# A two-layer diffusion backbone on one core: where the conditioning columns are summed

## The chip, the cores and the metric

One core of a Trainium2 chip (trn2) runs the whole program in one launch. The metric is the device time of one execution in microseconds, as the median of several runs. Less is better. Differences under 0.2% count as no change.

## What is computed

Two layers over 256 context tokens and 256 latent tokens of width 1024. Each layer normalises the tokens, shifts and scales them by conditioning columns, mixes them (attention, a gated delta network, a recurrent unit), merges the three branches, normalises and shifts again, and ends with a product-key expert layer. The conditioning columns are a matrix times two vectors, one for the latent and one for the context tokens:

```python
def adaln(cond, w, b):
    m = (jax.nn.silu(cond) @ w + b)[:, None, :]
    return jnp.split(m, N_MOD, axis=-1)

def modulate(h, shift, scale):
    return h * (1.0 + scale) + shift
...
for l in range(DEPTH):
    ml = adaln(c, w_ada[l], b_ada[l])
    mc = adaln(c_ctx[None, :], w_ada[l], b_ada[l])
    hl = modulate(rmsnorm(xl, norm1_g[l]), ml[0], ml[1])
    hc = modulate(rmsnorm(xc, norm1_g[l]), mc[0], mc[1])
    yc, yl = token_mixer(hc, hl, rope, l, need_ctx, w_in[l], ...)
    xl = xl + ml[2] * yl
```

`w_ada` is 1024 by 6144 for each layer. All of it is fp32. In the delta network each head pair needs the inverses of unit triangular matrices, and these are computed in the mixers too.

## The kernel before

**Layout.** Channels lie on the 128 partitions, tokens on the free axis. A product with a weight matrix goes by weight tiles of 128x1024 (`tblock`): a DMA brings the tile (`wraw`, three buffers), ScalarE rounds it to `wh`, VectorE forms the rest `wl` (line 97), and TensorE does 24 matmuls, three for each of eight chunks (lines 101 to 103).

**Conditioning.** One call of `ada` is called a block here. It makes 512 of the 6144 outputs of a layer for both vectors. It loads four tiles of 128x1024 fp32 (512 KB each) into `wraw`, does eight TensorE matmuls in which 32 columns of the padded vectors are the stationary side and 512 weight columns the moving side (line 185, spread over four groups of output partitions), copies the 128x512 result from PSUM with ScalarE (line 187), folds and turns it into columns with four small matmuls (line 190), and adds the bias (line 192). There are 24 blocks. Ten of them stand outside the mixers: four ahead of the first mixer, two ahead of the second, two behind each merge. Fourteen stand in the mixers, ten in layer 0 and four in layer 1.

**The mixers.** `mixer` weaves three streams of units: `g`, the delta network in four groups of two heads; `x`, the recurrent and the attention heads; and `f`, merge gates and conditioning blocks taken in turn. The table `RATE` says how many units of `x` and `f` follow each unit of `g`. The units are recorded in that order, and a scheduler then fixes the order of each engine's instructions. At run time every engine goes through its list in order, and so does the queue of DMAs issued from SyncE (SP).

**An inversion.** Each group of the delta network has one (`unit_inverse`). It writes diagonal 32x32 pieces of `W` to DRAM and reads them back in another layout (lines 677 and 681). Then come 60 small VectorE instructions, each of which needs the one before (lines 688 and 690). The result goes through DRAM again (lines 693 and 696) into `X`. Only then can `gdn_levels` start, whose first TensorE instructions are transposes of `X` (line 715). There are eight inversions, four in each layer. In what follows an inversion's chain is the stretch from its first to its last of the 60 instructions. The whole inversion is the stretch from the last product with `W` ahead of it (lines 594 and 595) to the first transpose of line 715.

Of the kernel before, what the change touches and what calls it, by code (L numbers as in the profile page):

```python
# [13 lines left out]
F32 = mybir.dt.float32  # L14
# [5 lines left out]
ALU = mybir.AluOpType  # L20
# [3 lines left out]
P = 128  # L24
# [15 lines left out]
class Net:  # L40
# [45 lines left out]
    th, nacc, nmm, l = None, 0, 0, 0  # L86
# [88 lines left out]
    def ada(self, l, b):  # L175
# [15 lines left out]
        m = slice(4 * b, 4 * b + 4)  # L191
        self.V.tensor_tensor(self.mods[:, l, m], pt, self.bada[:, l, m].unsqueeze(2).to_broadcast([P, 4, 2]), ALU.add)


    def norm_sums(self, pool, x, t0, ks):

        self.r = lambda shape=None, dt=F32: self.t(pool, shape or [P, NTOK], dt, "hr", 8)
        if ks[0] == 0:
            self.nss = self.acc()
        for k in ks:  # L200
            self.ssq(x[:, k, t0:], self.nss[:8, :NTOK - t0], self.selR[:, 7:15], k == 0, k == 7)
# [24 lines left out]
    def mixer(self, l, need):  # L226
        nc, V, S, T, I = self.nc, self.V, self.S, self.T, self.I
        self.l, self.need = l, need
        self.T0 = 0 if need else NC
        self.mgd = self.tc.dram_tile([P, 24, NTOK], F32, name=self.nm("mg"))  # L230
        self.ysd = [self.tc.dram_tile([P, 8, NTOK], F32, name=self.nm(f"ys{k}")) for k in range(3)]
        with ExitStack() as es:
            pool = lambda name: es.enter_context(self.tc.tile_pool(name=self.nm(name), bufs=1, reuse_waits="tile"))
            mp, ring = pool("mx"), pool("ring")
            self.r = lambda shape=None, dt=F32: self.t(ring, shape or [P, NTOK], dt, "t" + self.th, self.RING[self.th])
            self.rg = lambda: self.t(ring, [P, 4, P], F32, "rg", 4)
            self.th = "g"
            self.gdn_gates(mp, l)
            gp = pool("gdn")
            aes = ExitStack()  # L240
            ap = self.wextra = aes.enter_context(self.tc.tile_pool(name=self.nm("att"), bufs=1, reuse_waits="tile"))
            self.gated = set()
            gs = [lambda j=j: self.merge_gate(ring, l, j) for j in (*range(16, 24), *range(16))]
            ad = [lambda a=a: self.ada(*a) for a in ([(0, b) for b in range(4, 10)] + [(1, b) for b in range(4)] if l == 0 else [(1, b) for b in range(6, 10)])]
            g = self.gdn(gp, l)
            x = self.chain(*(u for h in range(8) for u in (self.lru_chunk(l, h), self.att_head(ap, l, h))),
                           self.merge_early(aes, pool, ring, l))
            f = self.chain(*(self.calls(us[i:i + 1]) for i in range(24) for us in (gs, ad)))
            self.weave(g, x, f)
            self.th = self.wextra = None  # L250

# [1180 lines left out]
```

## Time and profile before

| | |
|---|---|
| median of 3 runs | 4547.12 us (4546.77 to 4556.1) |
| the profiled execution | 4536.66 us |
| its span, first to last instruction | 4535.0 us |
| TensorE matmul busy | 4283.0 us, 94% |
| VectorE busy | 3214.4 us, 71% |
| ScalarE busy | 2348.0 us, 52% |
| first mixer, last instruction of its fourth inversion | 943.5 us |
| second mixer, its four inversions | 2737.5 to 3429.5 us |

The views used below are the page itself, the groups of instructions by line, windows (busy time of each engine in a stretch, its number of instructions, and the granted clock of TensorE as a share of full speed, where 1.00 is 2.4 GHz and 0.50 is 1.2 GHz), and the timeline. PE is TensorE's matmuls, PEld its weight loads, DVE VectorE, ACT ScalarE, POOL GpSimd.

### The profile page before, as it was taken

The numbers are of one execution on the slowest core, as the hardware profiler recorded it, in microseconds if no ns is written. First come the engines' busy times: TensorE is split into PE (matmuls) and PEld (weight loads), VectorE is DVE, ScalarE is ACT, GpSimd is POOL, SyncE is SP. The second block draws the span as 40 slices with busy tenths as digits, with TensorE's granted clock in tenths as the row PEclk, the third lists the DMA queues.
The fourth block names the chain that finished last, engine by engine and source line by source line (L and its number), as shares of the span: only waits on it lengthen the run. The fifth ranks groups of instructions, "written<-read, shape, count | busy, mean of one in ns | idle before, by whom it ended". The sixth has DMA issues, their size and how long they took to land.

```text
span 4535.0 us, 67054 instructions
## 1 busy us (share of the span) xinstructions
PE 4283.0 (94%) x24379; PEld 3612.7 (80%) x24379; DVE 3214.4 (71%) x7412; ACT 2348.0 (52%) x4145; POOL 457.7 (10%) x444
## 2 busy tenths in 40 slices
PE   7999999999889999999999989989998899999999
PEld 4686877777668999988888856878776789988888
DVE  4767576764459998677888766777775588656665
ACT  4555555553244688433333354656554357854444
POOL 0000000000000222333444200000000001100000
PEclk8999999999989999999999989999998999999999
DMA  4313222225632688899999734223221746677775
GB/s 152 121 59 109 70 96 86 96 73 175 205 107 91 235 275 294 320 333 336 338 340 333 251 121 140 84 84 98 66 89 57 236 149 208 228 266 243 242 248 182
DMA packets 364604, 820.69 MB, mean 181 GB/s; under 512 B 67184, under 2 KB 187504, under 8 KB 360944
## 3 DMA queue, kind: packets, MB, share of 16 engines
q1 hardware_dynamic: 315568, 614.00, 41.4%
q0 software_dynamic: 45824, 160.46, 9.7%
q10 hardware_dynamic: 2880, 41.94, 2.4%
q8 instruction: 191, 3.13, 0.3%
q14 instruction: 141, 1.16, 0.1%
HBM read 715.62 MB, written 100.66 MB: 180 GB/s over the span
## 4 chain that ended last, share of the span: by engine, by line
PE 81%; DVE 10%; ACT 4%; DMA 4%; issue 1%; SPq 0%; ACTq 0%; DVEq 0%
PE mm L103 11%; PE mm L101 11%; PE mm L102 11%; PE acx L101 4%; PE acx L102 4%; PE acx L103 4%; PE px L101 3%; PE px L102 3%; PE px L103 3%; DVE wl L97 2%; PE acg L103 1%; PE acg L101 1%; PE px L872 1%; PE acg L102 1%; PE pg L102 1%; PE pg L101 1%
## 5 line engine op out<-in xcount | busy, mean ns | idle before, releaser
L101 PE MATMUL mm<-hh,wh 128*128 128x256 f32 (+2 forms) x2784 | 916.2, 329 | 38.9 <-ACT wh L94 26.7
L103 PE MATMUL mm<-hh,wl 128*128 128x256 f32 (+2 forms) x2784 | 908.9, 327 | 18.6 <-DVE wl L97 18.3
L102 PE MATMUL mm<-hl,wh 128*128 128x256 f32 (+2 forms) x2784 | 903.5, 325 | 0.0
L94 ACT CAST wh<-wraw 128x1024 fp32r<-128x1024 f32 (+2 forms) x473 | 487.6, 1033 | 660.6 <-PE mm L102 525.2
L97 DVE TENSOR_TENSOR wl<-wraw,wh 128x1024 fp32r<-128x1024 f32 (+2 forms) x473 | 566.8, 1199 | 231.9 <-ACT wh L94 229.8
L101 PEld LDWEIGHTS mm<-hh,wh 128*128 128x128 f32 x2784 | 533.2, 192 | 68.9 <-ACT wh L94 28.5
L103 PEld LDWEIGHTS mm<-hh,wl 128*128 128x128 f32 x2784 | 531.9, 191 | 49.3 <-DVE wl L97 29.9
L102 PEld LDWEIGHTS mm<-hl,wh 128*128 128x128 f32 x2784 | 533.2, 192 | 22.9 <-issue 2.5
L97 DVE TENSOR_TENSOR vl<-vraw,vh 128x1024 fp32r<-128x1024 f32 x256 | 313.0, 1223 | 142.3 <-ACT vh L94 139.6
L94 ACT CAST vh<-vraw 128x1024 fp32r<-128x1024 f32 x256 | 269.0, 1051 | 274.4 <-PE pg L103 164.7
L94 ACT CAST pah<-ge 128x384 fp32r<-128x384 f32 (+1 forms) x256 | 114.7, 459 | 225.3 <-DVE ge L1196 172.0
L1160 DVE TENSOR_SCALAR ob<-cst,iT 128x128 f32<-128x128 f32 x640 | 183.3, 347 | 66.1 <-PE pg L1161 22.1
L1013 POOL DMA_DIRECT2D early<-ge x160 | 89.3, 558 | 1355.5 <-ACT ge L1006 952.3
L1218 POOL DMA_INDIRECT grow<-in_v,gix x128 | 179.5, 1403 | 259.4 <-DVE gacc L1233 229.6
L101 PE MATMUL mm<-hh,whx 128*128 128x512 f32 (+1 forms) x544 | 202.9, 373 | 2.9 <-ACT tx L800 1.8
L103 PE MATMUL mm<-hh,wlx 128*128 128x512 f32 (+1 forms) x544 | 200.9, 369 | 2.1 <-DVE wlx L97 2.1
L102 PE MATMUL mm<-hl,whx 128*128 128x512 f32 (+1 forms) x544 | 201.3, 370 | 0.0
L101 PE MATMUL px<-vh,pah 128*128 128x512 f32 x512 | 199.5, 390 | 0.0
L102 PE MATMUL px<-vl,pah 128*128 128x512 f32 x512 | 199.5, 390 | 0.0
L103 PE MATMUL px<-vh,pal 128*128 128x512 f32 x512 | 199.2, 389 | 0.0
L1218 POOL DMA_INDIRECT grow<-in_ur,gix x128 | 161.4, 1261 | 269.8 <-DVE gdot L1224 163.0
L1233 DVE SCALAR_TENSOR_TENSOR gacc<-grow,gdot,gacc 128x1024 f32<-128x1024 f32 x127 | 163.3, 1286 | 1.5
(518 smaller groups left out, 10030.3 us busy)
## 6 DMA issues: line engine op xcount, KB each, us to landing
wraw<-in_u SPq DMA_DIRECT2D x256, 512.0 KB
vraw<-in_v SPq DMA_DIRECT2D x256, 512.0 KB
wraw<-in_win SPq DMA_DIRECT2D x192, 512.0 KB
wraw<-in_wada SPq DMA_DIRECT2D x96, 512.0 KB
gate<-st ACTq DMA_DIRECT2D x20, 2048.0 KB
wraw<-in_wbr SPq DMA_DIRECT2D x48, 512.0 KB
pgt<-gate SPq DMA_DIRECT2D x32, 768.0 KB
wraw<-in_wq SPq DMA_DIRECT2D x32, 512.0 KB
```

The lines of the kernel that those rows point to most:

```text
L94: self.S.copy(h, src)
L97: return self.V.tensor_tensor(l, src, h.bitcast(F32), ALU.subtract)
L101: mm(out, lh, rh, start=first, stop=False)
L102: mm(out, lh, rl, start=False, stop=False)
L103: mm(out, ll, rh, start=False, stop=last)
L872: T.matmul(sc, a[s, q0:q0 + P], b[s, :nk], start=t == 0, stop=t == 2)
L1013: self.nc.gpsimd.dma_start(hd[j], self.expert_h(gl, l, j, T0, N))
L1160: ob = V.tensor_scalar(b, iota, iT[:, 1, n + k:n + k + 1], iT[:, 2, n + k:n + k + 1], ALU.is_equal, ALU.mult)
L1218: nc.gpsimd.indirect_dma_start(r, None, table, bass.IndirectOffsetOnAxis(ap=ix[:, k:k + 1], axis=0))
L1233: V.scalar_tensor_tensor(acc, r, dot[:, k:k + 1], acc, ALU.mult, ALU.add)
```

## The change

The fourteen blocks in the mixers no longer use `ada` but a new generator, `ada_steps`. It forms the products on VectorE: for each of the eight chunks of 128 rows and each of the two vectors, one instruction multiplies the 128x512 weight chunk by a column of one value per partition and adds the accumulator (the first of each vector only multiplies). That is 16 VectorE instructions a block, with two accumulators from the ring `tx` of nine buffers. TensorE then sums over the partitions with eight matmuls of one column each, and the bias is added as before. A block is recorded in two halves: the first with a merge gate in front of it, the second as the next unit of `f`. The ten blocks outside the mixers keep `ada`.

```diff
+    def ada_steps(self, l, b):
+
+        V, T = self.V, self.T
+        acc = [self.r([P, 512]) for _ in range(2)]
+        for k in range(4):
+            w = self.t(self.wp, [P, 2, 512], F32, "wraw", 3)
+            self.nc.sync.dma_start(w, self.I["wada"][l, b, k])
+            for i in range(2):
+                for c in range(2):
+                    f = self.cs[:, 2 * k + i, c:c + 1]
+                    if k + i == 0:
+                        V.tensor_scalar(acc[c], w[:, i], f, None, ALU.mult)
+                    else:
+                        V.scalar_tensor_tensor(acc[c], w[:, i], f, acc[c], ALU.mult, ALU.add)
+            if k == 1:
+                yield
+        pt = self.mm()[:, :8].rearrange("p (m c) -> p m c", c=2)
+        for m in range(4):
+            for c in range(2):
+                T.matmul(pt[:, m, c:c + 1], acc[c][:, m * P:(m + 1) * P], self.ones[:, :1], start=True, stop=True)
+        m = slice(4 * b, 4 * b + 4)
+        self.V.tensor_tensor(self.mods[:, l, m], pt, self.bada[:, l, m].unsqueeze(2).to_broadcast([P, 4, 2]), ALU.add)
+        yield
...
-            ad = [lambda a=a: self.ada(*a) for a in ([(0, b) for b in range(4, 10)] + [(1, b) for b in range(4)] if l == 0 else [(1, b) for b in range(6, 10)])]
+            ad = [self.ada_steps(*a) for a in ([(0, b) for b in range(4, 10)] + [(1, b) for b in range(4)] if l == 0 else [(1, b) for b in range(6, 10)])]
...
-            f = self.chain(*(self.calls(us[i:i + 1]) for i in range(24) for us in (gs, ad)))
+            f = []
+            for i, fn in enumerate(gs):
+                a = ad[i] if i < len(ad) else None
+                f += [lambda fn=fn, a=a: (fn(), next(a)), lambda a=a: next(a)] if a else [fn]
+            f = self.calls(f)
```

Since the engines' orders are fixed when the program is built, the change can be seen in them. First VectorE, in the middle of the chain of layer 0's second inversion, before. The rows of line 688 and 690 on `inv` are the chain, those of lines 874 to 882 attention, line 97 a weight or attention split:

```order
L688 TENSOR_TENSOR tg_3190<-inv_3189 64x234
L690 TENSOR_TENSOR inv_3189<-inv_3189,tg_3190 64x13x18
L882 SCALAR_TENSOR_TENSOR tx_3593<-tx_3597,asm_3582,tx_3593 128x512
L688 TENSOR_TENSOR tg_3190<-inv_3189 64x228
L690 TENSOR_TENSOR inv_3189<-inv_3189,tg_3190 64x12x19
L688 TENSOR_TENSOR tg_3190<-inv_3189 64x220
L690 TENSOR_TENSOR inv_3189<-inv_3189,tg_3190 64x11x20
L97 TENSOR_TENSOR al_3581<-px_3603,ah_3580 128x4x128
L688 TENSOR_TENSOR tg_3190<-inv_3189 64x210
```

And VectorE at the same links now (lines 688, 690 and 882 have become 716, 718 and 910, and line 207 is the new multiply-add):

```order
L716 TENSOR_TENSOR tg_3237<-inv_3236 64x234
L908 TENSOR_SCALAR asm_3700<-asm_3700,nlam_302 128x1
L718 TENSOR_TENSOR inv_3236<-inv_3236,tg_3237 64x13x18
L910 SCALAR_TENSOR_TENSOR tx_3711<-tx_3715,asm_3700,tx_3711 128x512
L716 TENSOR_TENSOR tg_3237<-inv_3236 64x228
L207 SCALAR_TENSOR_TENSOR tx_3767<-wraw_3769,csil,tx_3767 128x512
L718 TENSOR_TENSOR inv_3236<-inv_3236,tg_3237 64x12x19
L207 SCALAR_TENSOR_TENSOR tx_3768<-wraw_3769,csil,tx_3768 128x512
L716 TENSOR_TENSOR tg_3237<-inv_3236 64x220
L97 TENSOR_TENSOR al_3639<-px_3721,ah_3638 128x4x128
L718 TENSOR_TENSOR inv_3236<-inv_3236,tg_3237 64x11x20
L207 SCALAR_TENSOR_TENSOR tx_3767<-wraw_3775,csil,tx_3767 128x512
```

The new instructions stand singly between links that stood one behind the other.

Second, the SP queue at the end of the same inversion, before (`wada` is a block's tile, `win` a weight tile, `lw` the recurrent unit's weights, `dinv` and `X` the way back through DRAM):

```order
L121 DMA wraw_4127<-in_win 128x1024
L121 DMA wraw_4181<-in_win 128x1024
L121 DMA wraw_4228<-in_win 128x1024
L693 DMA dinv_3183<-inv_3189 64x1024
L121 DMA wraw_4266<-in_win 128x1024
L696 DMA X_3058<-dinv_3183 32x16x32 x4
```

And the SP queue there now (line 200 is the load of a new block, and lines 721 and 724 are the way through DRAM):

```order
L121 DMA wraw_4193<-in_win 128x1024
L121 DMA wraw_4247<-in_win 128x1024
L200 DMA wraw_4282<-in_wada 128x1024
L721 DMA dinv_3230<-inv_3236 64x1024
L927 DMA ys_97_421<-tx_3836 128x512
L200 DMA wraw_4288<-in_wada 128x1024
L724 DMA X_3105<-dinv_3230 32x16x32 x4
```

One weight tile fewer is fetched ahead of the chain's end, and a block's load stands where a weight tile's stood.

## Rows read from the trace of the kernel before

**Rows 1.** The page: busy time of an engine; shares of the last chain.
```profile
PE 4283.0 (94%) x24379; PEld 3612.7 (80%) x24379; DVE 3214.4 (71%) x7412; ACT 2348.0 (52%) x4145; POOL 457.7 (10%) x444
...
PE 81%; DVE 10%; ACT 4%; DMA 4%; issue 1%; SPq 0%; ACTq 0%; DVEq 0%
```
**Rows 2.** Windows: stretch, its length, busy us (instructions) by engine, clock, DMA.
```profile
360.00:380.00 20.00, 20.00 (x108) 15.75 (x108) 15.64 (x39) 13.99 (x26) 0.00 (x0) 1.00 0.29 93
420.00:440.00 20.00, 17.04 (x71) 8.68 (x70) 14.59 (x51) 6.30 (x16) 0.00 (x0) 0.91 0.41 145
3180.00:3200.00 20.00, 14.80 (x73) 12.37 (x72) 19.57 (x55) 6.80 (x12) 0.00 (x0) 0.83 0.29 92
```
**Rows 3.** Timeline of PE in one block: start, us to its end, instruction, idle before.
```profile
444.08 1.06 PE L185 MATMUL mm<-wraw,csil 128*32 128x512 f32 x6
...
448.91 1.05 PE L185 MATMUL mm<-wraw,csil 128*32 128x512 f32 x4 [0.42 <-DMA wraw<-in_wada]
450.65 1.05 PE L190 MATMUL mm<-fold,wl 128*128 128x2 f32 x8 [0.69 <-ACT wl L187]
```
**Rows 4.** Timeline of PE: wide matmuls, and one-column fp32 matmuls.
```profile
221.97 0.39 PE L101 MATMUL mm<-hh,wh 128*128 128x512 f32 x1
222.20 0.40 PE L102 MATMUL mm<-hl,wh 128*128 128x512 f32 x1
222.56 1.05 PE L454 MATMUL px<-ones,tx 128*128 128x1 f32 x8
```
**Rows 5.** Groups by line: busy us, mean ns, idle before, releasers.
```profile
L185 PE MATMUL mm<-wraw,csil 128*32 128x512 f32 x288 | 79.0, 721 | 15.6 <-DMA wraw<-in_wada 14.9 <-ACT tg L434 0.5 <-PE mm L1283 0.2
L190 PE MATMUL mm<-fold,wl 128*128 128x2 f32 x176 | 29.4, 288 | 11.8 <-ACT wl L187 11.7
```
**Rows 6.** Windows over the eight chains, first to last link.
```profile
184.40:224.20 39.80, 36.59 (x167) 25.07 (x166) 30.24 (x96) 15.21 (x31) 0.00 (x0) 0.91 0.44 140
419.80:459.00 39.20, 32.90 (x143) 18.88 (x143) 30.42 (x99) 14.58 (x32) 0.00 (x0) 0.91 0.43 146
663.10:705.30 42.20, 38.54 (x170) 23.65 (x169) 33.09 (x102) 17.23 (x37) 0.00 (x0) 0.88 0.50 169
905.30:943.50 38.20, 38.20 (x179) 28.46 (x178) 33.40 (x102) 19.21 (x40) 0.00 (x0) 1.00 0.30 97
2757.30:2795.20 37.90, 30.57 (x150) 21.30 (x151) 28.57 (x92) 11.30 (x19) 0.00 (x0) 0.82 0.53 174
2973.70:3010.20 36.50, 29.70 (x153) 23.64 (x152) 33.81 (x101) 13.58 (x25) 0.00 (x0) 0.86 0.29 97
3176.60:3209.50 32.90, 26.39 (x145) 22.31 (x144) 31.66 (x91) 17.96 (x27) 0.00 (x0) 0.90 0.32 98
3382.30:3414.60 32.30, 23.06 (x116) 19.40 (x116) 29.85 (x92) 15.44 (x26) 0.00 (x0) 0.84 0.16 54
```
**Rows 7.** Windows over whole inversions: the four with blocks, then the last.
```profile
169.10:237.70 68.60, 62.94 (x283) 42.87 (x284) 48.53 (x139) 26.70 (x51) 1.41 (x2) 0.93 0.49 140
400.70:473.70 73.00, 63.42 (x287) 42.45 (x287) 50.52 (x146) 27.16 (x51) 1.41 (x2) 0.93 0.49 151
648.80:718.60 69.80, 66.14 (x308) 45.78 (x307) 51.23 (x147) 26.42 (x51) 1.42 (x2) 0.93 0.46 142
2737.50:2810.70 73.20, 63.16 (x314) 43.42 (x314) 49.99 (x136) 27.35 (x46) 1.85 (x2) 0.91 0.56 175
3368.10:3429.50 61.40, 47.66 (x240) 39.80 (x239) 49.33 (x134) 27.16 (x44) 1.41 (x2) 0.83 0.26 74
```
**Rows 8.** Timeline of DVE in a chain without blocks, multiply-adds between links.
```profile
3190.12 0.40 DVE L688 TENSOR_TENSOR tg<-inv 64x238 f32<-64x238 f32 x1
3190.55 0.40 DVE L690 TENSOR_TENSOR inv<-inv,tg 64x238 f32<-64x238 f32 x1
...
3192.02 0.73 DVE L437 SCALAR_TENSOR_TENSOR tx<-tx,lcw,tx 128x508 f32<-128x508 f32 x1
3192.68 0.39 DVE L688 TENSOR_TENSOR tg<-inv 64x240 f32<-64x240 f32 x1
```

## The prediction

> **What bounds the kernel now.** I read the page first, then windows of 20 us through the mixers, the timelines at single blocks, and windows over the eight inversions. TensorE is busy 94% of the span and holds 81% of the last chain, VectorE 71% and 10% [rows 1]. Those are averages. In a plain stretch of the first mixer TensorE is busy all 20.00 of 20 us, at full clock, and VectorE 15.64 [rows 2]. There TensorE is the bound and VectorE has about a fifth to spare. At a block it is otherwise: 17.04 of 20 us busy, the clock at 0.91 [rows 2], with short waits for the tile (0.42 us) and for ScalarE's copy (0.69 us) [rows 3]. That is the loss that the blocks cause now. In the inversions of layer 1 that have no block beside them it is otherwise again: VectorE 19.57 of 20 us busy, TensorE 14.80 [rows 2]. Over whole chains VectorE is busy 33.81 of 36.50, 31.66 of 32.90 and 29.85 of 32.30 us there, 0.94 of the time on the mean, and 33.40 of 38.20 in layer 0's last [rows 6]. Such a chain is as long as its instructions on VectorE. In the four chains with blocks the share is only 0.73 to 0.78 of 39.80, 39.20, 42.20 and 37.90 us [rows 6], because TensorE, which also feeds the attention steps between the links, is busy with blocks and tiles. So each stage has its own bound: TensorE outside the inversions, nearly VectorE inside. The question is where the 224 new VectorE instructions stand.
>
> **Where they stand.** In VectorE's order 98 of the 224 lie inside four chains: 16, 30, 28 and 24 of them, in the first three inversions of layer 0 and the first of layer 1. The other four chains get none. The rest lie before and between.
>
> **Their price.** The trace has the same form in the same place: a multiply-add with a column as scalar over 508 fp32 elements, between two links. It is recorded as 0.73 us, and the next link starts 0.66 us after it began [rows 8]. Without it a link starts 0.43 us after the one before, 0.40 busy and 0.03 of waiting for its result [rows 8]; with it in between a link gives way after 0.33 (0.39 less the 0.07 that the multiply-add overlapped), so the net addition could be 0.55. I take 0.66 for each of the 16 instructions of a block, the two that only multiply too, since I count VectorE's busy time here. A block is then 10.6 us of VectorE. The Trainium skill, VectorE: DVE Perf Modes, the section on the TRN2 errata, gives 691 ns for a two-tensor fp32 instruction of 512 elements, and its tier table knows no faster mode for it, which speaks against this change. As an estimate, 98 instructions at 0.05 us less would put the forecast 5 us lower; the row is of the very form, so it decides.
>
> **Inside the four inversions: +29 us.** Chain by chain, VectorE's busy time now is 30.24, 30.42, 33.09 and 28.57 us [rows 6]. The moved instructions add 16, 30, 28 and 24 times 0.66: 10.6, 19.8, 18.5 and 15.8. Other rows enter and leave these chains in the new order (splits and attention steps, counted by form): +0.8, +0.5, -4.7 and +2.3. Sums: 41.6, 50.7, 46.9 and 46.7 us, together 185.9. At the share 0.94 of a VectorE-bound chain that is 198 us, against 159.1 now. Ahead of and behind a chain lie the ways through DRAM: 29.1 us in the last inversion (61.40 less 32.30), 125.5 in the four with blocks (284.6 less 159.1) [rows 6, 7]. I give 4 x 29 = 116 afterwards, so 9.5 come back. 198 - 159 - 9.5 = +29.
>
> **TensorE's work that no longer fits beside them: +52 us.** TensorE goes through its list in order, and the first transposes behind an inversion wait for it. What stands in the list between the group's last products and those transposes is all that TensorE can do meanwhile. Counted in the old order, the four inversions hold 129, 125, 159 and 72 weight-tile matmuls of 512 columns; in the new one 86, 84, 64 and 48. The reason is visible in the queues: the tiles of the blocks occupy the three `wraw` buffers for as long as VectorE works on them, and VectorE has fewer splits between the links. 203 matmuls at 0.23 us [rows 4] are 47 us, and some attention matmuls worth 5 us leave too. The 52 us have to be done in stretches where TensorE is busy 20.00 of 20 us, so they add their full length.
>
> **What the blocks give back on TensorE: -9 us.** At full clock a block costs about 3.5 us for its eight matmuls, in groups of about 1.05 us recorded, and 0.9 for the fold [rows 3]. The new sums are eight fp32 matmuls of one column, sixteen passes, and eight passes stand at 1.05 us recorded [rows 4], 0.9 to the next start: 1.8 us. 2.6 us less a block, 37 for fourteen. But 28 of these 37 lie in the four inversions, where TensorE would then stand idle anyhow; 9 count. The Trainium skill, TensorE: Matmul & The Clock Gate, section Back-to-back issue gap, has about 25 ns as the floor of a matmul of 1 to 64 columns. By that, an estimate, the sums would take 0.4 us a block and the fourteen 20 us less; the row, with its weight load for every pass, says 0.11 a pass, and I go by the row.
>
> **Waits: -7 us, order: +3 us.** Waits for tiles and for the copy are 15.6 and 11.8 us in the two larger groups [rows 5], about 1.5 us a block with the smaller ones. Five of the fourteen blocks stand outside the inversions: -7. Those inside are in the lengths above. The third inversion of layer 1 gets nine more VectorE instructions between its links (91 to 100) and grows by some 7 us, others shrink by 4: +3. Nothing is taken for ScalarE's 14 copies and the freed PSUM bank: ScalarE is busy 52% [rows 1]; it could be up to 0.7 us a block [rows 3], 10 us, which I keep for the low end. Two of nine `tx` buffers are held by accumulators; what that delays is already in the order.
>
> **Sum.** +29 +52 -9 -7 +3 = +68. The profiled execution took 4536.66 us (span 4535.0), 10.5 under the median of 4547.12; on its own scale that is 4605, on the median's 4615. I predict 4615 us, 1.5% slower.
>
> **Rivals.**
> A, faster: the moved instructions cost the chains nothing, because VectorE has 9 us of idle time in each of the four [rows 6] and the attention steps come sooner once TensorE is free. Then no +29 and no +52; 37 us of TensorE work and 14 x 1.5 = 21 us of waits go. The clock of 0.91 to 0.93 in these inversions [rows 7], about 10 us at 1.2 GHz in each, costs TensorE 20 us and would go as well: 4547 - 78 = 4469. It decides if the new instructions fit in the idle time: 9 us against 10.6 to 19.8. Against it stands that they do not, in three of four.
> B, a little slower: the inversions grow by 29, but the displaced 52 us find idle time of TensorE outside. 4547 + 29 - 9 - 7 + 3 = 4563. Against it: 20.00 of 20 busy [rows 2].
> C, much slower: VectorE waits for the blocks' tiles in the chain, as TensorE does now, with the links and the splits queued behind it in order, and TensorE behind the splits; and SP holds a block's load ahead of the way back into `X`. If the share of busy time stays at 0.77 as in the chains with blocks now, they take 185.9 / 0.77 = 241 us, 43 more: 4658. The clock works in the same direction: in the last inversion, with TensorE busy 47.66 of 61.40 us, it is 0.83 [rows 7], and the new inversions leave TensorE less work. The skill's clock page says the same in general, that rest throttles and activity releases the clock; it changes no number here.
> That the change does not do what it says can be left out: the orders show the instructions.
>
> **How the numbers follow.** Forecast 0.54, within 20 us of 4615. A 0.10, B 0.12, C 0.18, and 0.06 for something between A and B that ends as no change. 0.2% is about what a measurement of this kernel can tell from none, so slower means over 4556: 0.84, same 0.06, faster 0.10. Low end: net price 0.55 (-11), ScalarE's copies (-10), chains fully packed (-12), half of B's relief (-26): 4556, rounded to 4560. High end: C, 4660. A lies outside, and a little of C.
>
> **What would show it.** Right: the four inversions at 70 to 84 us instead of 68.6 to 73.2, VectorE over 90% busy in their chains, TensorE at about half in them with a clock of 0.85 or less; stretches between inversions longer by some 10 to 25 us, with TensorE full; the other half of the program unchanged. Wrong: chains of 40 us with more on VectorE (A), stretches between that do not grow (B), or VectorE idle in the chains for `wraw` (C). The forecast would be wrong at its root if TensorE's list were not what holds it, that is, if it were busy in the new inversions.

## The result, and the profile after

The changed kernel takes 4663.99 us (median of 4 runs, 4662.06 to 4672.01) against 4547.71 us before: 1.0257 times as long, 95% interval 1.0242 to 1.0272. It is slower, as forecast, but by 116 us and not by 68, and the time lies 4 us above the high end of the range. The profiled execution took 4662.78 us, span 4661.1; that of before was 11 us under its median, so that the two traces differ by 126 us.

The page of the kernel after, the rows that answer to [rows 1]: busy time by engine, and shares of the last chain.

```profile
PE 4302.3 (92%) x24267; PEld 3662.3 (79%) x24267; DVE 3335.6 (72%) x7636; ACT 2346.4 (50%) x4132; POOL 463.3 (10%) x444
...
PE 75%; DVE 14%; ACT 5%; DMA 4%; issue 1%; SPq 0%; POOL 0%; ACTq 0%; DVEq 0%; POOLq 0%
```

VectorE is busy 121 us longer and holds 14% of the last chain instead of 10%. TensorE has 112 instructions fewer and is nevertheless busy 19 us longer: it runs more at half clock. To see where, the spans were cut into stretches by the same landmarks (last product ahead of a chain, first transpose behind it). First windows of the kernel after over the four inversions with blocks, then over the four stretches that follow them. Columns as in [rows 2]: stretch, length, busy us (instructions) of TensorE, weight loads, VectorE, ScalarE and GpSimd, clock, DMA share, GB/s.

```profile
170.50:240.90 70.40, 49.45 (x209) 37.88 (x208) 57.05 (x165) 18.07 (x38) 1.41 (x2) 0.71 0.32 93
442.40:525.90 83.50, 55.05 (x216) 41.51 (x215) 63.31 (x167) 24.37 (x47) 1.41 (x2) 0.71 0.34 101
712.30:794.10 81.80, 51.08 (x190) 39.65 (x191) 60.43 (x165) 20.02 (x41) 1.62 (x2) 0.62 0.33 96
2828.60:2906.90 78.30, 48.94 (x243) 40.34 (x243) 64.18 (x156) 19.00 (x33) 1.94 (x2) 0.74 0.41 123
...
240.90:442.40 201.50, 198.32 (x1103) 160.97 (x1101) 143.05 (x309) 110.62 (x212) 1.81 (x1) 0.96 0.25 82
525.90:712.30 186.40, 182.67 (x1048) 148.89 (x1046) 130.15 (x289) 107.30 (x207) 1.82 (x1) 0.98 0.21 70
794.10:988.90 194.80, 193.67 (x1109) 158.31 (x1108) 136.11 (x302) 111.94 (x215) 1.81 (x1) 0.99 0.23 77
2906.90:3084.10 177.20, 171.56 (x1108) 146.85 (x1108) 125.81 (x279) 111.08 (x211) 1.81 (x1) 0.97 0.29 96
```

And the same four following stretches of the kernel before, which are not among the rows ahead of the prediction:

```profile
237.70:400.70 163.00, 162.89 (x966) 131.31 (x964) 117.26 (x262) 101.63 (x202) 1.81 (x1) 1.00 0.18 61
473.70:648.80 175.10, 173.63 (x1008) 138.52 (x1007) 118.98 (x266) 105.43 (x205) 1.81 (x1) 1.00 0.21 71
718.60:890.20 171.60, 168.92 (x994) 135.19 (x993) 116.84 (x263) 106.08 (x207) 1.80 (x1) 1.00 0.21 71
2810.70:2959.00 148.30, 147.97 (x974) 126.95 (x974) 105.46 (x243) 98.67 (x194) 1.80 (x1) 0.98 0.25 81
```

The inversions themselves [rows 7] have grown by 29 us in sum (284.6 to 314.0). The larger part, 102 us, is behind them (658.0 to 759.9), where TensorE has 426 instructions more (3942 to 4368). In the inversions TensorE's instructions fell from 1192 to 858 and its clock from 0.91 to 0.93 down to 0.62 to 0.74.

For each stretch TensorE's share was then taken apart: the work (its busy time, with what ran at 1.2 GHz counted half), what half clock added (the other half), and the idle rest. Worked out from the two traces, after less before, in us:

| | length | work | half clock | idle |
|---|---|---|---|---|
| four inversions with blocks | +29.3 | -88.7 | +37.4 | +80.5 |
| four stretches behind them | +102.0 | +77.7 | +15.1 | +9.1 |
| rest of the two mixers, up to the last inversion | -2.2 | -33.2 | +10.1 | +20.9 |
| merge, experts, and behind the last inversion | -2.6 | -2.8 | +3.7 | -3.5 |
| all | +126 | -47 | +66 | +107 |

TensorE has 47 us less to do, and the kernel takes 126 us longer.

### The profile page after: what moved, and what is told of

Its sections match the earlier page's. It is cut to its first block, busy times and chain, and to the rows that moved or that the text cites. A ratio compares the mean times of both kernels' runs of the same rounds, so it can differ in the third digit from the quotient of the medians.

```text
span 4661.1 us, 67060 instructions
## 1 busy us (share of the span) xinstructions
PE 4302.3 (92%) x24267; PEld 3662.3 (79%) x24267; DVE 3335.6 (72%) x7636; ACT 2346.4 (50%) x4132; POOL 463.3 (10%) x444
## 4 chain that ended last, share of the span: by engine, by line
PE 75%; DVE 14%; ACT 5%; DMA 4%; issue 1%; SPq 0%; POOL 0%; ACTq 0%; DVEq 0%; POOLq 0%
PE mm L103 11%; PE mm L101 11%; PE mm L102 11%; PE acx L101 3%; PE acx L103 3%; PE acx L102 3%; PE px L101 3%; PE px L102 3%; PE px L103 3%; DVE wl L97 2%; PE px L900 1%; PE acg L103 1%; PE acg L101 1%; PE acg L102 1%; DVE tx L207 1%
## 5 line engine op out<-in xcount | busy, mean ns | idle before, releaser
L101 PE MATMUL mm<-hh,wh 128*128 128x256 f32 (+3 forms) x2888 | 960.8, 333 | 45.8 <-ACT wh L94 34.8
L103 PE MATMUL mm<-hh,wl 128*128 128x256 f32 (+3 forms) x2888 | 957.4, 332 | 23.9 <-DVE wl L97 21.4
L102 PE MATMUL mm<-hl,wh 128*128 128x256 f32 (+3 forms) x2888 | 951.2, 329 | 0.0
L101 PEld LDWEIGHTS mm<-hh,wh 128*128 128x128 f32 (+1 forms) x2888 | 555.2, 192 | 81.3 <-ACT wh L94 38.1
L103 PEld LDWEIGHTS mm<-hh,wl 128*128 128x128 f32 (+1 forms) x2888 | 554.1, 192 | 57.4 <-DVE wl L97 33.2
L102 PEld LDWEIGHTS mm<-hl,wh 128*128 128x128 f32 (+1 forms) x2888 | 554.8, 192 | 29.7 <-issue 3.9
L101 PE MATMUL mm<-hh,whx 128*128 128x512 f32 (+1 forms) x472 | 179.1, 379 | 8.7 <-ACT whx L94 8.0
L102 PE MATMUL mm<-hl,whx 128*128 128x512 f32 (+1 forms) x472 | 176.8, 375 | 0.0
L103 PE MATMUL mm<-hh,wlx 128*128 128x512 f32 (+1 forms) x472 | 176.4, 374 | 0.0
```

Of the source, the lines that this page charges most:

```text
L101: mm(out, lh, rh, start=first, stop=False)
L102: mm(out, lh, rl, start=False, stop=False)
L103: mm(out, ll, rh, start=False, stop=last)
```

## Experiments: VectorE's time, or something that is held

The theory on record was VectorE's time in the inversions and, for the displaced work, the three `wraw` buffers that are held. The rivals were the hand-over between VectorE and TensorE, and the clock. In the tables below, the last two columns are the growth of the four inversions and of the four stretches behind them, in us against the trace of before.

**Short multiply-adds.**

```diff
-                        V.scalar_tensor_tensor(acc[c], w[:, i], f, acc[c], ALU.mult, ALU.add)
+                        V.scalar_tensor_tensor(acc[c][:, :64], w[:, i, :64], f, acc[c][:, :64], ALU.mult, ALU.add)
```

> The multiply-adds work on 64 of the 512 columns only, so seven eighths of the products are left out; the number of instructions, the tiles, the hand-over to TensorE and the sums stay. If the loss is VectorE's time in the inversions, 196 instructions fall from 0.73 us to 0.1 to 0.2, some 110 us of VectorE come back, and the time falls to about that of the kernel before: 4510 to 4560 us. If the loss is the hand-overs (TensorE waits 43.5 us for the last product, VectorE 20.9 us for the sums), it stays at 4620 us or more.

**Sums one unit later.**

```diff
             if k == 1:
                 yield
+        yield
         pt = self.mm()[:, :8].rearrange("p (m c) -> p m c", c=2)
...
-                f += [lambda fn=fn, a=a: (fn(), next(a)), lambda a=a: next(a)] if a else [fn]
+                q = ad[i - 1] if 0 < i <= len(ad) else iter("x")
+                f += [lambda fn=fn, a=a, q=q: (fn(), next(q), next(a)), lambda a=a: next(a)] if a else [lambda fn=fn, q=q: (fn(), next(q))]
```

> The sums of a block and its bias are recorded one unit of f later, at the start of the next block's first half. If the hand-overs make the loss, most of the 43.5 and 20.9 us of waits go and the time falls by 40 to 60 us, to 4605 to 4625. If VectorE's time makes it, TensorE only waits elsewhere: 4650 to 4670 us.

**Mixed.** `self.kind` is the kind of the unit of `g` that is being recorded.

```diff
         V, T = self.V, self.T
+        if self.kind == "inv":
+            yield
+            self.ada(l, b)
+            yield
+            return
```

> A block whose turn comes while the delta network records an inversion is done by TensorE as before; four blocks, all in layer 0 between the inversions, use the multiply-adds on VectorE. If the loss comes from VectorE's time inside the inversions, four blocks outside cost nothing and give back 2.6 us of TensorE and 1.5 us of waits each: 4525 to 4547 us. If every block costs the same wherever it stands (117 us over 14 is 8.3 each), the time is 4547 + 33 = 4580 us.

**Filler on TensorE.**

```diff
             for i in range(2):
+                T.matmul(self.mm()[:32], self.cs[:, 2 * k + i], w[:, i], start=True, stop=True)
                 for c in range(2):
```

> The multiply-adds and sums stay, and TensorE does eight matmuls of 32 by 512 on the same weight tiles in addition, into banks that nobody reads (3.5 us a block at full clock, 49 us in all). If the granted clock is a cause by itself (66 us more are lost at 1.2 GHz than before), the added work raises it in the inversions and the time stays or falls: 4635 to 4665 us. If the clock only follows TensorE's idleness and TensorE's list is what counts, up to 49 us are added: 4680 to 4715 us.

| | median us | ratio to before (interval) | inversions | behind them |
|---|---|---|---|---|
| changed kernel | 4664.0 | 1.0257 (1.0242 to 1.0272) | +29 | +102 |
| short multiply-adds | 4621.8 | 1.0159 (1.0131 to 1.0187) | +1 | +79 |
| sums one unit later | 4655.5 | 1.0235 (1.0206 to 1.0263) | +30 | +88 |
| mixed | 4565.3 | 1.0037 (1.0023 to 1.0051) | -6 | +41 |
| filler | 4716.1 | 1.0378 (1.0346 to 1.0409) | +44 | +103 |

Short multiply-adds take the 29 us off the inversions and 42 us off the time, but they leave 75 us standing: the work is displaced as before (-92 us in the inversions, +74 behind them). In the four inversions VectorE is then busy 198 us, as before (200), and its extra time there is gone. So VectorE's time is a cause, and not of the larger part. By its number alone, 4622 us would also fit the hand-overs (4620 or more). But the sums' waits are nearly free: TensorE's and VectorE's waits for each other there fell from 43.5 and 20.9 to 27.3 and 11.0 us, and the time by 8. (The 43.5 counts weight loads and matmuls that stood still at the same time; the matmuls alone waited 5.7 + 13.5 = 19.2 us. By lines, busy us, mean ns, idle before:)

```profile
L207 DVE SCALAR_TENSOR_TENSOR tx<-wraw,csil,tx 128x512 f32<-128x512 f32 x196 | 141.7, 739 | 0.0
L213 PE MATMUL acx<-ones,tx 128*128 128x1 f32 x128 | 20.3, 283 | 5.7 <-DVE tx L207 5.7
L213 PE MATMUL mm<-ones,tx 128*128 128x1 f32 x96 | 18.4, 314 | 13.5 <-DVE tx L207 13.5
```

The filler costs 52 us, but it added far more than the 49 us that the expectation counted. All its matmuls write the same 32 output partitions, and they do not run side by side. By lines (line 202 is the filler), and one place at full clock:

```profile
L202 PE MATMUL mm<-wraw,csil 128*32 128x512 f32 x146 | 79.2, 638 | 5.7 <-DMA wraw<-in_wada 5.6
L202 PE MATMUL acx<-wraw,csil 128*32 128x512 f32 x78 | 46.9, 687 | 3.3 <-DMA wraw<-in_wada 2.7 <-ACT mth L342 0.5
```
```profile
459.40 1.88 PE L202 MATMUL mm<-wraw,csil 128*32 128x512 f32 x4
```

Four records take 1.88 us here, and 1.05 where `ada` spreads them over four groups of output partitions [rows 3]. At full clock the filler is 110 us of work. Against the changed kernel TensorE has 111 us more work, 57 us less idle time and 7 us less at half clock. In the inversions its clock rises only to 0.75 to 0.87, and they grow by 15 us instead of shrinking. So about half of the filler went into idle time, and the clock gave back 7 us, far less than the filler costs. What half clock costs by itself this run can't tell, and no other run tests it apart.

The mixed kernel missed both expectations, and its trace showed why. Its loss stands in the first inversion and behind it (TensorE's work -20.8 there, +27.3 behind), although no multiply-add is in that chain, which runs from 184.7 to 219.6 us. SP's loads of the block's tiles (line 205 there is the load, 210 and 212 the products), and VectorE's products of them:

```profile
176.80 7.97 SPq L205 DMA_DIRECT2D wraw<-in_wada  x2
186.80 0.33 SPq L349 DMA_DIRECT2D mg<-mth  x1
187.22 0.38 SPq L121 DMA_DIRECT2D wraw<-in_win  x1
195.47 0.33 SPq L807 DMA_DIRECT2D wraw<-in_lw  x1
196.50 0.33 SPq L349 DMA_DIRECT2D mg<-mth  x1
200.92 0.33 SPq L205 DMA_DIRECT2D wraw<-in_wada  x1
```
```profile
224.10 0.88 DVE L210 TENSOR_SCALAR tx<-wraw,csil 128x512 f32<-128x512 f32 x2
224.89 4.06 DVE L212 SCALAR_TENSOR_TENSOR tx<-wraw,csil,tx 128x512 f32<-128x512 f32 x6
```

Two tiles lie in `wraw` from 185 us, a third from 201; VectorE has them behind the chain in its list and starts at 224. One weight tile (`win`) is fetched between 187 and 224 us, and none from 201 on; in the kernel before, five are fetched between 207 and 219. So the next theory was that the blocks hold the ring.

## Experiments: the rings

**Buffers of their own** for the blocks' tiles in layer 0, as halves of 128x512, three of them (layer 1's memory has no room): in the changed kernel, in the kernel before, and in the mixed one. In the kernel before, the edit is made in `ada`. For layer 1 the two removed lines stay.

```diff
-            w = self.t(self.wp, [P, 2, 512], F32, "wraw", 3)
-            self.nc.sync.dma_start(w, self.I["wada"][l, b, k])
             for i in range(2):
+                w = self.t(self.wextra, [P, 1, 512], F32, "wada", 3)
+                self.nc.sync.dma_start(w, self.I["wada"][l, b, k, :, i:i + 1])
...
```

> In layer 0 the blocks' tiles no longer go through the three buffers of wraw but, as halves of 128x512, through three buffers of their own; layer 1 is left as it is. If the loss is that the blocks' tiles hold wraw while VectorE works through them, weight tiles flow again in layer 0's first three inversions: TensorE's work in them rises from 33 to 39 us at full clock to 50 or more, and of the 96 us that layer 0's mixer grew by, half or more goes: 4585 to 4620 us. If VectorE's time or its order alone makes the loss, the time stays at 4640 to 4665 us.

> The kernel before, with the same buffers of their own for the blocks in layer 0's mixer: TensorE's matmuls free a tile soon after it lands, so the ring theory has little to give here: 4525 to 4550 us. If the buffers help whatever engine reads the tiles, this falls by as much as the kernel with multiply-adds does, 40 us or more: under 4510 us.

> As the mixed kernel (four blocks of layer 0 outside the recorded inversions on VectorE, ten on TensorE), and those four with buffers of their own. Its loss of 18 us stood in the first inversion, where a block's tiles held all of wraw until VectorE had done the chain. If that is the cause, the loss goes and some 4 us a block come back: 4525 to 4550 us. If VectorE's time is the cause, it stays at 4560 to 4570 us.

**High priority**: the sixteen products of a block under `with self.tc.high_priority():`.

> The scheduler is told to put the multiply-adds first: the sixteen of a block then stand in one piece in VectorE's order, not singly between links. The buffers come free sooner if the tiles are there in time, but VectorE then waits in its list for the tiles. If holding wraw is what counts, TensorE's work in the inversions rises and the time falls to 4600 to 4640 us; if VectorE's time in the chain counts, each of the blocks delays its chain by its whole 10.6 us and its tiles' waits: 4665 to 4720 us.

| | median us | ratio to before (interval) | inversions | behind them |
|---|---|---|---|---|
| own buffers | 4658.0 | 1.0242 (1.0219 to 1.0265) | +36 | +76 |
| before, own buffers | 4568.3 | 1.0046 (1.0032 to 1.0060) | +9 | +8 |
| mixed, own buffers | 4568.6 | 1.0041 (1.0028 to 1.0054) | 0 | +27 |
| high priority | 4704.9 | 1.0338 (1.0303 to 1.0373) | +49 | +70 |

The ring alone is not it. TensorE's list shows what happened: between the last product and the first transpose, layer 0's first three inversions hold 129, 125 and 159 matmuls of weight tiles before, 86, 84 and 64 in the changed kernel, and 120, 92 and 82 with own buffers. Of these only the first is nearly back. High priority frees the ring no sooner (54, 81 and 72) and puts the products in the chains' way. The mixed kernel, expected at 4525 to 4550 us if the ring were its loss, did not move either. For the kernel before, own buffers are a loss of 21 us, which was not expected, and it is no clean control of the ring: with tiles that come in halves the matmuls of line 185 seldom run side by side, and in layer 0's mixer they take 64 us of TensorE where they took 41.

What else does a block hold? Its sum takes a PSUM bank in the rotation `mm`, `mm`, `acx`, through which the weight tiles go too, and with the sum waiting for sixteen products the rotation stands. With the sums in one of the attention's two banks and own buffers together, the lists hold 125, 124 and 124; with the bank alone 86, 79 and 75.

**The sums' bank**, alone and with own buffers in layer 0; then with short multiply-adds, and with layer 1's blocks back on TensorE.

```diff
-        pt = self.mm()[:, :8].rearrange("p (m c) -> p m c", c=2)
+        pt = self.px()[:, :8].rearrange("p (m c) -> p m c", c=2)
```

> Only the PSUM bank of the sums is changed: they go into one of the attention's two banks (px) and not into the rotation mm and acx, in which weight tiles are summed. TensorE's list in layer 0's first three inversions then still has only 79 or so weight-tile matmuls on the mean (86, 84 and 64 in the changed kernel, 129, 125 and 159 in the kernel before), because wraw is still held. If two rings together keep the weight tiles out, and one is not enough, the time stays: 4650 to 4670 us. If the bank is the cause by itself, 4600 to 4625 us.

> Both: the blocks' tiles have buffers of their own in layer 0, and the sums (in both layers) go into the attention's banks. TensorE's list in those three inversions has 125, 124 and 124 weight-tile matmuls again. If the two rings displaced TensorE's work, the stretches between layer 0's inversions, 73 us longer now, shrink by 40 to 60 us: 4595 to 4625 us. If VectorE's time is the cause, TensorE only waits longer in the inversions: 4645 to 4670 us.

> As the kernel with both rings freed, with the multiply-adds on 64 of 512 columns (seven eighths of the products are left out). If VectorE's time and the rings are two separate causes, the 42 us that shorter multiply-adds gave before come off again: 4555 to 4585 us. If they overlap, the two together give less than their sum: 4590 us or more.

> As the kernel with both rings freed in layer 0, and layer 1's four blocks back on TensorE as before. Layer 1's mixer grew by 36 us, most of it in its first inversion and the stretch behind it; that goes: 35 us less than with layer 1 on VectorE, 4560 to 4590 us. If layer 0 with both rings freed costs nothing, 4547 us or less.

| | median us | ratio to before (interval) | inversions | behind them |
|---|---|---|---|---|
| bank alone | 4690.8 | 1.0326 (1.0295 to 1.0357) | +40 | +96 |
| bank, own buffers in layer 0 | 4660.3 | 1.0261 (1.0234 to 1.0289) | +36 | +58 |
| the same, short multiply-adds | 4601.8 | 1.0130 (1.0107 to 1.0152) | 0 | +34 |
| the same (512 columns), layer 1 on TensorE | 4615.7 | 1.0152 (1.0122 to 1.0182) | +38 | +33 |

Both rings freed bring most of TensorE's work back where it stood: behind layer 0's first three inversions the growth falls from 73 to 31 us. Yet the time did not fall, and the theory's 4595 to 4625 us was missed by 35 us. The inversions did not shrink, and layer 1, which shared `wraw` still, lost by the attention's banks (its last three inversions together +23 us, +12 in the changed kernel). The bank alone, which was expected to change nothing or to help, costs 27 us. Layer 1's four blocks make 45 us of the loss; with them back on TensorE 4560 to 4590 us were expected, so layer 0 alone costs 26 us more than the theory had room for.

**Layer 1 with room.** One pair of `wh` and `wl` less in layer 1's mixer makes room for own buffers in both layers. The kernel before and the changed one with that edit alone are the controls.

```diff
-        nx = (1, 3)[self.l] if self.wextra else 0
+        nx = (1, 2)[self.l] if self.wextra else 0
```

> Control: the kernel before with two instead of three extra pairs of wh and wl buffers in layer 1's mixer. A small loss in layer 1 if the third pair was used: 4545 to 4565 us.

> Control: the changed kernel with the same edit. It should move by as much as the kernel before does with it: 4660 to 4685 us.

> The changed kernel with that edit and with buffers of their own for the blocks' tiles in both layers. If holding wraw is what empties TensorE at the start of layer 1's mixer and in its first inversion (35 us less work at full clock there, +22 in the stretch behind), that stretch and the start come back by 15 us or more, besides some 6 us in layer 0: 4625 to 4650 us. If VectorE's order is what holds them, within 10 us of the control.

> The same with the sums in the attention's banks too. In layer 0 this brought 24 us against the changed kernel. If the two rings act together in layer 1 as well, its mixer loses half of its 43 us: 4615 to 4640 us. If the attention's banks cost in layer 1 what they seemed to cost before (with the bank alone changed the time rose by 27 us), 4650 us or more.

> Own buffers for the blocks' tiles in both layers, sums in the rotation, multiply-adds on 64 of 512 columns (seven eighths of the products are left out). The buffers alone gave 23 us and shorter multiply-adds alone 42: if they are separate causes, 4664 - 65 = 4599 us, within 10. If VectorE's time only matters because it holds the tiles, about 4622 us as with shorter multiply-adds alone.

> The same with the sums in the attention's banks. If rings and VectorE's time are all there is, this comes to within 25 us of the kernel before: 4547 to 4575 us. If something else holds TensorE (waits for the sums, the attention's banks), 4590 us or more.

| with the edit | median us | ratio to before (interval) | inversions | behind them |
|---|---|---|---|---|
| before | 4551.3 | 1.0013 (0.9998 to 1.0029) | +2 | +4 |
| changed kernel | 4661.5 | 1.0258 (1.0228 to 1.0288) | +31 | +98 |
| own buffers | 4638.6 | 1.0211 (1.0180 to 1.0242) | +44 | +54 |
| own buffers, bank | 4653.5 | 1.0242 (1.0213 to 1.0271) | +50 | +46 |
| own buffers, short multiply-adds | 4608.5 | 1.0140 (1.0114 to 1.0165) | +15 | +42 |
| own buffers, bank, short multiply-adds | 4579.6 | 1.0077 (1.0054 to 1.0100) | +22 | -3 |

Here the causes separate. The rings displace the work: behind the inversions TensorE has 73 us more to do in the control, 74 with short multiply-adds, and 19 with own buffers and the bank. VectorE's time makes the inversions long: short multiply-adds bring them from +29 to +1, or from +50 to +22 with the rings freed. And the two hang together: in time the rings alone give 8 us against the control, short multiply-adds alone 42 against the changed kernel, and both 82 against the control. Freed rings hardly help as long as the multiply-adds are whole, since what they give behind the inversions (+98 to +46) is taken back in part inside them (+31 to +50), and in layer 1's other inversions (+28 in those three, +13 in the control). VectorE's rows in layer 1's first inversion show with what; by lines, count and busy us. The changed kernel:

```profile
L207 DVE SCALAR_TENSOR_TENSOR tx<-wraw,csil,tx 128x512 f32<-128x512 f32 x36 | 25.6, 738 | 0.0
...
L97 DVE TENSOR_TENSOR wl<-wraw,wh 128x1024 fp32r<-128x1024 f32 x3 | 3.7, 1221 | 5.1 <-ACT wh L94 5.1
L97 DVE TENSOR_TENSOR wlx<-wraw,whx 128x1024 fp32r<-128x1024 f32 x3 | 3.6, 1209 | 0.0
```

The kernel with own buffers and the other bank:

```profile
L207 DVE SCALAR_TENSOR_TENSOR tx<-wada,csil,tx 128x512 f32<-128x512 f32 x42 | 31.0, 743 | 0.0
...
L97 DVE TENSOR_TENSOR wl<-wraw,wh 128x1024 fp32r<-128x1024 f32 (+1 forms) x5 | 5.6, 1113 | 0.0
L97 DVE TENSOR_TENSOR wlx<-wraw,whx 128x1024 fp32r<-128x1024 f32 x4 | 4.9, 1214 | 0.0
```

Each weight tile that gets through needs its split on VectorE, 1.2 us: 9 splits for 6, and six more multiply-adds fall into this inversion. Over the four inversions VectorE is then busy 264 us, and 245 in the changed kernel; these 19 us are about what the inversions have grown by (21). Thirteen of them are splits (30 for 18), while the multiply-adds are as many (135 for 136). The sums of the windows over the four inversions (length, then busy time as above) of the kernel with own buffers and bank, and of the same with short multiply-adds:

```profile
sum 334.80, PE 243.40 PEld 189.28 DVE 264.43 ACT 85.11 POOL 5.91; mean PE 60.85 PEld 47.32 DVE 66.11 ACT 21.28 POOL 1.48
```
```profile
sum 306.80, PE 250.04 PEld 194.37 DVE 213.28 ACT 96.14 POOL 6.08; mean PE 62.51 PEld 48.59 DVE 53.32 ACT 24.04 POOL 1.52
```

What is left of the last kernel, 30 us, is in the inversions: +22 in the four, and another +32 in the last three of layer 1, partly given back in between. Those three have no blocks. The sums' bank makes about half of it: that edit and no other brings the three from +12 to +27 (bank alone beside the changed kernel) and from +14 to +28 (own buffers with and without it). How it does so, where no block stands, is open. No version beats the kernel before. The best complete one in which all fourteen blocks are on VectorE takes 4638.6 us, and even leaving seven eighths of the products out does not reach 4547.

## Why the prediction came out too low

**The price: near, a little high.** A multiply-add in a chain is recorded at 0.73 to 0.74 us, and the next link starts 0.66 us after it began, as in [rows 8]. The timeline of VectorE in the second inversion:

```profile
492.27 0.37 DVE L718 TENSOR_TENSOR inv<-inv,tg 64x220 f32<-64x220 f32 x1
492.57 0.74 DVE L207 SCALAR_TENSOR_TENSOR tx<-wraw,csil,tx 128x512 f32<-128x512 f32 x1
493.23 0.36 DVE L716 TENSOR_TENSOR tg<-inv 64x210 f32<-64x210 f32 x1
```

The link ahead of it gives way after 0.30 of its 0.37 us. So one multiply-add adds 0.59 us to VectorE's busy time and not the 0.66 that the sum took; over 98 of them that is 7 us. The prediction had this overlap for its low end.

**Inside the four inversions: right, in part by luck.** +29 was forecast and +29.3 measured. The chains, which answer to [rows 6]:

```profile
185.90:227.00 41.10, 22.19 (x76) 15.38 (x75) 38.65 (x116) 12.66 (x29) 0.00 (x0) 0.57 0.21 70
455.20:511.60 56.40, 36.50 (x128) 27.78 (x129) 47.30 (x137) 14.42 (x30) 0.00 (x0) 0.59 0.31 103
725.50:776.40 50.90, 27.58 (x102) 20.39 (x98) 44.14 (x131) 13.71 (x30) 0.00 (x0) 0.57 0.26 83
2844.80:2892.80 48.00, 31.48 (x164) 24.81 (x162) 44.28 (x120) 12.48 (x21) 0.16 (x2) 0.78 0.31 101
```

They take 196.4 us where 198 were forecast, and VectorE bounds them nearly. But it is busy 174.4 us (185.9 forecast) at a share of 0.89 (0.94), and these two errors cancel. In the second chain it stands idle for 9 us; there it waits 5 us for other matmuls of TensorE and 3 for the new sums, whose wait on VectorE had no term. Rival C's mechanism, a share of 0.77, did not occur, although its 4658 us came nearest. (In the four chains before the share is 0.75 to 0.78 by [rows 6], not 0.73 to 0.78.) Rivals A and B are refuted by the chains and by the stretches behind them, which grew by 11 to 39 us where 10 to 25 were named as the sign.

**The displaced work: right in size, the cause incomplete.** Outside the four inversions TensorE has 77.7 - 33.2 - 2.8 = 41.7 us more work; the two terms on record, +52 and -9, make 43. The cause on record, `wraw` held and fewer splits between the links, was a part of it. The prediction took a PSUM bank as freed; the bank of the sums, which held the second and third inversion's tiles back when `wraw` was free (92 and 82 in the list), was left out. Fewer splits were not the reason for most of it, since with both rings freed the three lists are nearly full again (373 matmuls, 413 before and 234 in the changed kernel) beside whole multiply-adds.

**The waits: the step that failed.** On record, -7 us outside the inversions, and no term for the clock. Measured there: idle +26.5 us and half clock +28.9. With the work these are the 97 us outside; the forecast had 39. (Of the clock's part some 15 us may belong to the single executions, by the last point of this document; the idle part does not change so.) Seventeen of the idle us stand at the starts of the two mixers (4.8 and 12.7), where blocks stand that had been counted as outside and without cost. The last 48 us ahead of the second mixer's first inversion, after:

```profile
2780.00:2828.60 48.60, 32.54 (x168) 27.18 (x166) 39.78 (x101) 31.30 (x53) 0.00 (x0) 0.79 0.18 57
```

and before:

```profile
2689.00:2737.50 48.50, 45.87 (x264) 35.46 (x264) 37.07 (x93) 35.49 (x61) 0.00 (x0) 0.93 0.28 95
```

The stretch is as long as it was, with 96 TensorE instructions fewer, at 57 GB/s for 95: the tiles do not come, and the work is done later, behind the inversion. With own buffers and the bank this start has all its work again (+0.2 us for -16.0). The blocks outside the inversions were thus priced (-9 and -7 us) as if nobody would wait for VectorE outside a chain. VectorE has 22% to spare in a plain stretch [rows 2], but its list is in order and the tiles are held until their turn. That the clock falls with TensorE's work was said under rival C, and not carried into the sum. The half clock outside stands in pieces: 8.5 us behind the first inversion, 6.6 behind the other three, 7.1 at the two starts, the rest thinly spread. Behind the second and the third inversion the clock is at 1.00 from the start; over the first 19 us behind the first it is 0.73, and behind the fourth 0.91. What each piece costs in time no run shows apart.

**The sums** were priced at 1.8 us a block. That holds at full clock (2860.8 to 2862.6 us); at half clock a block's sums take 4.0, with two weight matmuls between them (2891.4 to 2895.4 us), and 38.7 / 14 = 2.8 on the mean. The order's +3 was nearer to +8: layer 1's last three inversions grew by 12 us, and the stretches between them shrank by 4.

## What to carry to other kernels

When work moves from an engine that frees its inputs at once to one that takes them singly between other things, count how long each buffer and each PSUM bank is held, and who goes through the same ring behind it. TensorE's list between two fixed points can be read from the order before any run; if it shrinks, the work comes back later, here at full length and with idle time and half clock beside it. Freeing a ring paid here only once the engine behind it had time for what then got through.

## What the hardware showed

- An eighth of the columns does not take an eighth of the time: the multiply-add is recorded at 0.737 us (median) on 512 columns and at 0.276 us on 64. That is 1.03 ns a column and 0.21 us a piece. The Trainium skill, VectorE: DVE Perf Modes, section on the TRN2 errata, has a fixed cost per instruction beside a cost per element; as an estimate its formula for two fp32 tensors gives 0.224 and 0.691 us, 0.05 less than each row here, with the same slope.
- Matmuls with 32 stationary columns run side by side when they write different groups of output partitions: at full clock four records take 1.05 us [rows 3], and 1.88 us in the filler, where all write the same group.
- Layer 0's mixer with the same lists of instructions differed by 14 us between two profiled executions (bank and own buffers, with layer 1 on VectorE and on TensorE: +63 and +77 us against before), by the granted clock alone (15 us more at half clock, the same work and idle time within 2 us). Differences of that size between single traces say nothing.
